# Down projection in seven products for 40 of 44 feature tiles, with a half piece last whose sums stay on chip, and all weight sums formed in memory during attention

## The chip, the core and the metric

The kernel runs on one core of a Trainium2 chip, in one launch. The metric is device microseconds of that core, lower is better. PE is the matrix engine, DVE the vector engine, ACT the scalar engine, POOL the GpSimd engine and SP the engine that here only issues transfers. All arithmetic is on 4-byte floats; each large product is made of three matmuls of split operands (below).

## The reference

One layer of a streaming encoder on x of 512 tokens by 2048 columns: a norm, a joint q/k/v projection, 16 attention heads of three kinds, an output projection with residual, a norm, a gated MLP of width 5632, a residual and a last norm. What the change touches is the last product:

```
    x = x + jnp.einsum('bse,ed->bsd', y, w_o[l])                    # attention's output, residual
    h = rmsnorm(x, ffn_norm[l])
    g = causal_dwconv(jnp.einsum('bsd,df->bsf', h, w_gate[l]), conv_w[l], conv_b[l])
    u = jnp.einsum('bsd,df->bsf', h, w_up[l])
    x = x + jnp.einsum('bsf,fd->bsd', jax.nn.silu(g) * u, w_down[l])   # "down", 5632 -> 2048
return rmsnorm(x, final_norm)
```

## The kernel before

**Split products.** Each operand is split into a high part (`wh`, a cast on ACT) and a remainder (`wl`, a subtraction on DVE). `mm3` (L67) makes a product of three matmuls: high by remainder, remainder by high, high by high. A "step" below is the work with one pair `wh`, `wl` of 128 by 1024 weights.

**Stages.** Attention runs 16 heads ("slots" 0 to 15). Each head ends in `finish`, which stores its output (`y_dram`) on POOL's queue. The output projection follows, then gate and up, tile by tile over 44 feature tiles, of which 40 use a seven-product scheme of their own (`strassen`), then down.

**Down.** The 44 feature tiles of 128 are 11 chunks of `CH` = 4. A *piece* of 4 chunks (2 pairs `b` of chunks) is multiplied in Strassen's manner: the 2 by 2 blocks are chunk of a pair by token half on the features' side, and chunk of a pair by column group `g`, `g+1` on the weights' side. Seven products `n` = 1 to 7 take the place of eight. The sums on the features' side are formed during gate/up and stored (`ab_dram`, `t_dram`); those on the weights' side are formed here. `NSEV` = 32 gives two pieces, and each is worked off in two *units* `Seven(c, g)`, `g` = 0 and 2. A unit has 14 products (7 `n` by 2 `b`) of two steps each, 28 steps, and a step has 12 matmuls of 512 columns (`multiply`).

**Order in this stage.** It is written by hand for all engines. In iteration `k`, `parts` casts and subtracts the weights of step `k`; between the cast and the subtraction stands `prepare(k+1)`, the addition (if any) that the next step's source needs; `prepare_6` forms the operand of product 6 (`s2`, tiles `sh`, `sl`); then come the matmuls of step `k`, and `sums(k)`, which reads finished accumulators. `wh` and `wl` have three buffers (`wspl`), so the cast of step `k` can start when step `k-3` is done. The raw weights have four buffers, in `rw` and `wraw`. Accumulators: `r1` and `r6` in the four `acc` banks, `r5` and `r7` in the four `att` banks, which the later products `dn` use as well.

**Weight sums.** Only the first unit (`self.formed`) finds sums ready-made, in `s_dram`: POOL's queue writes four tiles of 1 MB in attention, each by a copy (slots 0 to 3) and an accumulating transfer onto it (slots 4 to 7), memory to memory. The other three units add on DVE, eight additions each.

**Result sums.** `sums` builds each unit's four output blocks in tiles `e` and `U` (pool `ep`, one buffer each) and `put` stores them to one memory tensor per piece, `c_dram[0]` and `c_dram[1]`. Chunks 8 and 9 are then plain products (`down`, 192 matmuls of 512 columns each), added into the residual `x2` by `plus`. Between their groups of four output tiles the generator `turned` loads the stored sums of both pieces, adds them (DVE), transposes them on PE (16 transposes to a group) and adds them to `x2`. Chunk 10 is a plain product too, made in two token halves of 256 columns; the last norm of the first half runs under the second. `gated(c, n)` loads and splits a plain chunk's features (`ah`, `al`).

Of the kernel before, what the change touches and what calls it, by code (L numbers as in the profile page):

```python
# [24 lines left out]
NSEV = 32  # L25
# [18 lines left out]
def trunk(ctx, tc, xT, wqkv, wo, wo15, wgu, wd, par, lam4, rel, out):  # L44
# [72 lines left out]
    s_dram = [dram.tile([P, 2048], F32, name=f"s_dram{i}") for i in range(4)]  # L117
    c_dram = [dram.tile([P, NB, D], F32, name=f"c_dram{i}") for i in range(NSEV // 16)]
# [123 lines left out]
    with ExitStack() as actx:  # L242
# [172 lines left out]
        def finish(o, summer, n, eps, gain, slot):  # L415

            sq = tmp.tile([P, S], F32, tag="t2", name="osq")
            act.activation(sq, o, AF.Square)
# [13 lines left out]
            if slot >= KT - 2:  # L432
                pending.append(last)
            else:
                stored = pool.dma_start(y_dram[:, slot, :], o).ins
                if slot < 8:

                    i = slot % 4
                    b, w = divmod(i, 2)
# [55 lines left out]

        def chunk_pair(p, qkh, vs):
            ws = []
            for c in range(2):
                bias = tmp.tile([P, S], F32, tag="bias", name="rbias", bufs=2)
                pool.dma_start(bias, rel[2 * p + c])  # L500
# [3 lines left out]
                for i in reversed(range(NB)):  # L504
# [7 lines left out]
                    yield 2  # L512
            yield 3
# [163 lines left out]
        for n in range(NH - 2):  # L677
            if n == 7:
                far_masks()
            weave(n, following(n), 48, 8 if n == 0 else 0)  # L680
# [318 lines left out]
    with ExitStack() as actx:  # L999
# [52 lines left out]
        def features(c, i):  # L1052

            n, b = ORDER[i]
# [17 lines left out]
        def weights(src):  # L1072
            raws[0] += 1
            raw = (rw, wraw)[raws[0] % 2].tile([P, 2048], F32, tag="raw", name="raw")
            sync.dma_start(raw, src)
            return [raw.rearrange("p (m i c) -> p m i c", m=4, i=4)[:, :, 2 * h : 2 * h + 2, :] for h in range(2)]
# [4 lines left out]
        class Seven:  # L1081


            def __init__(self, c, g, fs):
                self.c, self.g, self.fs = c, g, fs
                self.banks, self.s2 = {}, {}
                self.formed = c == g == 0

            def load(self):
                c, g = self.c, self.g  # L1090
                w = {}
                for b in range(2):
                    w["11", b] = weights(wd[c + 2 * b, g])
                    if self.formed:
                        w["22", b], w["21", b] = [weights(s_dram[2 * b + s]) for s in range(2)]
                    else:
                        w["21", b], w["22", b] = [weights(wd[c + 2 * b + i, g + 1]) for i in range(2)]
                for b in range(2):
                    w["12", b], w["x22", b] = [weights(wd[c + 2 * b + 1, g + j]) for j in range(2)]
                self.w = w  # L1100

            def prepare(self, k):
# [3 lines left out]
                n, b = ORDER[k // 2]  # L1106
                h, w = k % 2, self.w
                a = {key: w[key, b][h] for key in ("11", "21", "22", "12", "x22")}
                if n in (1, 2, 4):
                    self.src = a[{1: "11", 2: "12", 4: "x22"}[n]]  # L1110
                elif n == 6:
                    self.src = self.s2[b][h]
                else:
                    s2 = self.s2[b][h] if n == 3 else None
                    dst, x, y = {
                        5: (a["22"], a["21"], a["22"]),
                        7: (a["21"], a["21"], a["11"]),
                        3: (s2, s2, a["12"]),
                    }[n]
                    if n == 3 or not self.formed:  # L1120
                        add(dst, x, y)
                    self.src = dst

            def prepare_6(self, k):

                n, b = ORDER[k // 2]
                h, w = k % 2, self.w
                if n == 7:
# [14 lines left out]
            def multiply(self, k):  # L1143
                n, b = ORDER[k // 2]
# [6 lines left out]
                for i in range(2):  # L1151
                    o, w = (2 * h + i) * HS, slice(i * S, (i + 1) * S)
                    for t in range(2):
# [6 lines left out]
                            b == h == i == 1,  # L1160
# [9 lines left out]

            def sums(self, k):

                r = self.banks
                if k == 12:
# [3 lines left out]
                elif k == 17:  # L1178
# [4 lines left out]
                elif k == 18:  # L1183
# [3 lines left out]
                elif k == 26:  # L1187
# [4 lines left out]
                elif k == 28:  # L1192
# [4 lines left out]
                elif k == 30:  # L1197
# [4 lines left out]
        c0 = NSEV // CH  # L1202
        NSTEP = 2 * len(ORDER)
        fs = [{} for _ in range(0, c0, 4)]
        units = [Seven(c, g, fs[c // 4]) for c in range(0, c0, 4) for g in (0, 2)]
# [4 lines left out]
        at = {s: (0, i) for i, s in FIRST.items()}  # L1210
        for n in range(1, len(fs)):
            at.update({(2 * n - 1) * NSTEP + s: (n, i) for i, s in NEXT.items()})
# [3 lines left out]
        def load_features():  # L1216
            if wanted:
                n, i = wanted.pop(0)
                loaded.append(features(4 * n, i))

        def split_features(n, i):
            fs[n][ORDER[i]] = feature_parts(i, loaded.pop(0))
# [14 lines left out]
        with tc.manual_schedule(engines={E.PE, E.DVE, E.Activation, E.SP, E.Pool}):  # L1237
# [4 lines left out]
            for s in range(len(units) * NSTEP + 3):  # L1242
                u, k = divmod(s, NSTEP)
                if u < len(units):
                    v, q = divmod(s + 1, NSTEP)
                    units[u].parts(lambda: units[v].prepare(q) if v < len(units) else None)
                    if v < len(units):
                        units[v].prepare_6(q)
                    units[u].multiply(k)
                if u > 0:  # L1250
                    units[u - 1].sums(k + NSTEP)
                if u < len(units):
                    units[u].sums(k)
                if s in at:
                    split_features(*at[s])
                    if at[s] > (0, 3):
                        load_features()
                if u == len(units) - 1 and k in (18, 21, 24, 26):
                    load_residual((18, 21, 24, 26).index(k))
# [5 lines left out]
        def turned():  # L1265

            yield
            for g in range(4):
                cs = []
                for c in c_dram:  # L1270
                    cs.append(rw.tile([P, NB, S], F32, tag="raw", name="cs"))
                    sync.dma_start(cs[-1], c[:, :, g * S : (g + 1) * S])
                for c in cs[1:]:
                    dve.tensor_tensor(out=cs[0], in0=cs[0], in1=c, op=ALU.add)
                for mm in range(4):
                    x = x2[4 * g + mm]
                    bank = acc_bank("ct")
                    for t in range(NB):
                        pe.transpose(
                            out=bank[:, t * P : (t + 1) * P], in_=cs[0][:, t, mm * P : (mm + 1) * P], identity=ident  # L1280
# [55 lines left out]

        kept = [pair(n, name="k") for n in range(8)]
# [74 lines left out]
```

## Time and profile before

| what | value |
|---|---|
| runs shown | 2204.95, 2206.73, 2207.64 us; median 2206.73 |
| the profiled execution | 2206.56 us, of which the span of its trace is 2204.8 and 1.76 lie outside the span |
| PE | busy 2173.9 us of the span, 99% |
| DVE, ACT, POOL | busy 73%, 49%, 13% |
| gate/up in seven products | 924.9 to 1741.1 us |
| down in seven products (4 units) | 1741.1 to 2049.7 us |
| down, plain chunks 8 and 9 | 2049.7 to 2143.8 us |
| down, chunk 10 in two halves | 2143.8 to 2190.4 us |
| the end (last norm, stores) | 2190.4 to 2204.8 us |

Times are positions in the span. A busy PE is a PE whose queue of matmuls doesn't run dry; the clock granted to it is 1.00 in every stage but the end. "Idle before, and what ended it" in a group names who was waited for.

### The profile page before, as it was taken

To read this page: it belongs to the slowest core of one execution; us is meant where nothing else is said; L and a number is where in the kernel's file an instruction comes from. 1 tells how busy PE (TensorE), PEld (TensorE's weight loads), DVE (VectorE), ACT (ScalarE), POOL (GpSimd) and SP (SyncE) were. 2 spreads that over 40 slices of the span, in tenths; PEclk is the share of its full clock that TensorE was granted. 3 is DMA by queue.
4 is the path that set the end of the run, shared out by engine and by line. 5 is a ranking of instruction groups with operands and counts; after the bars stand their busy time and mean duration, and the time that the engine had idled before them with its cause. 6 is when DMAs were issued, how large, how long until landed. Compare 5 with 4: busy or idle time off the path is not lost.

```text
span 2204.8 us, 34927 instructions
## 1 busy us (share of the span) xinstructions
PE 2173.9 (99%) x13916; PEld 1984.3 (90%) x13916; DVE 1604.0 (73%) x2277; ACT 1071.9 (49%) x1566; POOL 292.5 (13%) x531
## 2 busy tenths in 40 slices
PE   8999999999999999999999999999999999999997
PEld 7889888898888888799999999999999978888887
DVE  6665666877677547877777777787777788887675
ACT  5555555777565224444444444444444554544232
POOL 0100101000112221111111111111111010000003
PEclk9999999999999999999999999999999999999999
DMA  5332434222234445877787788778777665556742
GB/s 196 109 111 101 124 101 123 89 84 89 98 119 163 165 145 185 274 233 221 193 239 217 196 227 225 205 212 224 196 200 189 224 225 195 201 200 232 264 172 77
DMA packets 98163, 388.14 MB, mean 176 GB/s; under 512 B 11408, under 2 KB 20368, under 8 KB 81040
## 3 DMA queue, kind: packets, MB, share of 16 engines
q1 hardware_dynamic: 65728, 269.90, 35.9%
q0 software_dynamic: 30976, 114.84, 20.4%
q8 instruction: 109, 1.79, 0.3%
q10 hardware_dynamic: 1296, 1.17, 0.2%
q14 instruction: 54, 0.44, 0.1%
HBM read 341.30 MB, written 52.95 MB: 179 GB/s over the span
## 4 chain that ended last, share of the span: by engine, by line
PE 95%; DMA 2%; DVE 2%; issue 1%; ACT 0%; SPq 0%; DVEq 0%; POOLq 0%; ACTq 0%
PE c L67 36%; PE r L67 12%; PE v L67 8%; PE q L67 8%; PE k L67 8%; PE wo L67 8%; PE dn L67 6%; PE g L67 2%; PE u L67 2%; PE tr L395 1%; DMA f<-t_dram 1%; PE pv L67 1%; PE sc L360 1%; PE sc L359 1%; PE pv L410 0%
## 5 line engine op out<-in xcount | busy, mean ns | idle before, releaser
L61 DVE TENSOR_TENSOR wl<-a,wh 128x1024 fp32r<-128x1024 f32 x199 | 243.4, 1223 | 176.2 <-ACT wh L60 175.9
L67 PE MATMUL c<-bl,wh 128*128 128x256 f32 x1280 | 363.7, 284 | 4.3 <-ACT wh L60 4.3
L67 PE MATMUL c<-bh,wl 128*128 128x256 f32 x1280 | 363.6, 284 | 0.7 <-DVE wl L61 0.7
L67 PE MATMUL c<-bh,wh 128*128 128x256 f32 x1280 | 363.4, 284 | 0.0
L60 ACT CAST wh<-a 128x1024 fp32r<-128x1024 f32 x199 | 209.0, 1050 | 242.5 <-DVE a L873 207.2
L60 ACT CAST wh<-raw 128x1024 fp32r<-128x1024 f32 (+1 forms) x163 | 168.6, 1035 | 257.2 <-PE wo L67 88.7
L67 PE MATMUL c<-h2l,wh 128*128 128x256 f32 x960 | 272.0, 283 | 1.4 <-DVE U L899 0.9
L67 PE MATMUL c<-h2h,wh 128*128 128x256 f32 x960 | 271.8, 283 | 0.0
L67 PE MATMUL c<-h2h,wl 128*128 128x256 f32 x960 | 271.8, 283 | 0.0
L67 PEld LDWEIGHTS c<-bl,wh 128*128 128x128 f32 x1280 | 246.9, 193 | 4.6 <-ACT wh L60 4.5
L67 PEld LDWEIGHTS c<-bh,wl 128*128 128x128 f32 x1280 | 246.9, 193 | 1.0 <-DVE wl L61 1.0
L67 PEld LDWEIGHTS c<-bh,wh 128*128 128x128 f32 x1280 | 246.9, 193 | 0.0
L61 DVE TENSOR_TENSOR wl<-raw,wh 128x1024 fp32r<-128x1024 f32 (+1 forms) x163 | 197.0, 1211 | 64.8 <-ACT wh L60 64.2
L67 PEld LDWEIGHTS c<-h2l,wh 128*128 128x128 f32 x960 | 184.4, 192 | 1.8 <-DVE U L899 1.1
L67 PEld LDWEIGHTS c<-h2h,wl 128*128 128x128 f32 x960 | 184.4, 192 | 0.0
L67 PEld LDWEIGHTS c<-h2h,wh 128*128 128x128 f32 x960 | 184.4, 192 | 0.0
L67 PE MATMUL r<-wl,fh 128*128 128x512 f32 x448 | 174.8, 390 | 2.8 <-DVE wl L1140 2.8
L67 PE MATMUL r<-wh,fl 128*128 128x512 f32 x448 | 174.4, 389 | 0.0
L67 PE MATMUL r<-wh,fh 128*128 128x512 f32 x448 | 174.3, 389 | 0.0
L67 PE MATMUL v<-wl,hh 128*128 128x256 f32 x512 | 148.0, 289 | 8.2 <-DVE wl L61 8.2
L67 PE MATMUL v<-wh,hh 128*128 128x256 f32 x512 | 146.3, 286 | 0.0
L67 PE MATMUL v<-wh,hl 128*128 128x256 f32 x512 | 146.2, 286 | 0.0
(305 smaller groups left out, 5180.4 us busy)
## 6 DMA issues: line engine op xcount, KB each, us to landing
a<-in_wgu SPq DMA_DIRECT2D x121, 512.0 KB, 5.9
raw<-in_wd SPq DMA_DIRECT2D x48, 1024.0 KB, 5.7
raw<-in_wqkv SPq DMA_DIRECT2D x46, 1024.0 KB, 4.8
z<-in_wgu SPq DMA_DIRECT2D x80, 512.0 KB, 5.6
z<-in_wgu POOLq DMA_DIRECT2D x78, 512.0 KB, 9.3
raw<-in_wo SPq DMA_DIRECT2D x16, 1024.0 KB, 4.9
raw<-in_wgu SPq DMA_DIRECT2D x8, 1024.0 KB, 4.9
ab_dram<-g POOLq DMA_DIRECT2D x32, 256.0 KB, 6.4
```

The lines of the kernel that those rows point to most:

```text
L60: a = act.copy(out=hi, in_=src)
L61: d = dve.tensor_tensor(out=lo, in0=src, in1=hi.bitcast(F32), op=ALU.subtract)
L67: pe.matmul(o, l[x], r[y], start=start and i == 0, stop=stop and i == 2, skip_group_check=on)
L359: pe.matmul(bank[:, kt], q[c][:, qt], k[c][:, kt], start=True, stop=False)
L360: pe.matmul(bank[:, kt], q[c][:, qt], kh[c][:, kt], start=False, stop=not strict)
L395: pe.transpose(out=bank[:, (i - j) * P : (i - j + 1) * P], in_=w[:, o : o + P], identity=ident)
```

## The change

`NSEV` goes from 32 to 40: chunks 8 and 9 become a third piece with one pair of chunks (`nb` = 1), whose two units have 7 products, 14 steps each. The plain chunks are gone, and chunk 10 alone is left.

- **Weight sums.** All six units read their sums from `s_dram`, now 20 tiles. The copies are issued on ACT's queue, two in each of slots 0 to 9, and the accumulating transfers on POOL's queue, two in each of slots 2 to 11. The loads of the band heads' bias move from POOL's queue to ACT's and are issued ahead (`load_bias`). The additions in `prepare` for products 5 and 7 are gone; those for 6 and 3 stay.
- **Order of products.** With two pairs the last products go 2, 2, 3, 3, 4, 4 where they went 2, 3, 4, 2, 3, 4. With one pair the order is 1, 6, 5, 7, 2, 3, 4.
- **Result sums.** `c_dram` is one tensor; the second piece's `put` accumulates onto the first's. The half piece's units don't store: `load_sums` brings the sums so far into tiles `c_last`, and `last_sums` adds the accumulators to these, the first copy of `r1` on ACT.
- **End.** The weights of chunk 10's first group are loaded and split within the last unit. Two groups of transposes (32) run right behind the last unit, the other two between the groups of chunk 10's first half.

```diff
-NSEV = 32
+NSEV = 40
...
+    s_parts = {}
+    for c in range(0, NSEV // CH, 2):
+        for g in (0, 2):
+            s_parts[c, g, 1] = (c + 1, g + 1), (c, g + 1)
+            s_parts[c, g, 3] = (c, g), (c, g + 1)
...
+                keys = list(s_parts)
+                with tc.issue_after(squared):
+                    for key in keys[2 * slot : 2 * slot + 2]:
+                        act.dma_start(s_dram[key], wd[s_parts[key][0]])
+                if slot >= 2:
                     with tc.issue_after(stored):
-                        if slot < 4:
-                            pool.dma_start(s_dram[i], wd[2 * b, 0] if w else wd[2 * b + 1, 1])
-                        else:
-                            pool.dma_start(s_dram[i], wd[2 * b, 1], accum_op=ALU.add, max_dma_last_dim=8192)
+                        for key in keys[2 * slot - 4 : 2 * slot - 2]:
+                            pool.dma_start(s_dram[key], wd[s_parts[key][1]], accum_op=ALU.add, max_dma_last_dim=8192)
...
-        ORDER = [(n, b) for b in range(2) for n in (1, 5, 7, 6)] + [(n, b) for b in range(2) for n in (2, 3, 4)]
+        def order_of(nb):
+            first = (1, 6, 5, 7) if nb == 1 else (1, 5, 7, 6)
+            return [(n, b) for b in range(nb) for n in first] + [(n, b) for n in (2, 3, 4) for b in range(nb)]
+
+        PIECES = [(c, min(4, NSEV // CH - c) // 2) for c in range(0, NSEV // CH, 4)]
...
+                self.read = dict(zip((12, 17, 18, 23, 27, 30), range(6)))
...
-                if n in (1, 2, 4):
-                    self.src = a[{1: "11", 2: "12", 4: "x22"}[n]]
-                elif n == 6:
+                if n == 6:
                     self.src = self.s2[b][h]
+                elif n == 3:
+                    s2 = self.s2[b][h]
+                    add(s2, s2, w["12", b][h])
+                    self.src = s2
                 else:
...
-                    if n == 3 or not self.formed:
-                        add(dst, x, y)
-                    self.src = dst
+                    self.src = w[{1: "11", 2: "12", 4: "x22", 5: "22", 7: "21"}[n], b][h]
...
-                pool.dma_start(c_dram[self.c // 4][:, 2 * t : 2 * t + 2, col], e)
+                pool.dma_start(c_dram[:, 2 * t : 2 * t + 2, col], e, accum_op=ALU.add if self.c else ALU.bypass)
...
+            def load_sums(self, row):
+
+                g = self.g + row
+                for t, e in reversed(list(enumerate(pair((1, 2, 3, 9)[g], F32, "c")))):
+                    c_last[g, t] = e.rearrange("p (t c) -> p t c", t=2)
+                    pool.dma_start(c_last[g, t], c_dram[:, 2 * t : 2 * t + 2, g * S : (g + 1) * S])
+
+            def last_sums(self, k):
+                r = self.banks
+
+                def onto(row, t, n=None):
+                    e = c_last[self.g + row, t]
+                    if n is None:
+                        add(e, self.U, e)
+                    else:
+                        for i in range(2):
+                            add(e[:, i, :], r[n][i], e[:, i, :])
+
+                if k == 2:
+                    self.U = fe.tile([P, 2, S], F32, tag="f", name="U")
+                    for i in range(2):
+                        act.copy(out=self.U[:, i, :], in_=r["1"][i])
+                elif k == 4:
+                    for i in range(2):
+                        add(self.U[:, i, :], r["6"][i], self.U[:, i, :])
+                sums = {
+                    5: (1, 1),
+                    6: (1, 1, "5"),
+                    7: (0, 1),
+                    8: (1, 1, "7"),
+                    9: (1, 0),
+                    12: (0, 0, "1"),
+                    13: (0, 1, "5"),
+                    14: (1, 0, "7"),
+                }
+                if k in sums:
+                    onto(*sums[k])
...
+                if u == len(units) - 1 and k == 4:
+                    kept[0] = [pair(n, name="k") for n in (5, 6)]
+                    raw_last = next_raw(wd[NCH - 1, 0])
+                if u == len(units) - 1 and k in (12, 13):
+                    split(*kept[0][k - 12], raw_last[:, (k - 12) * 1024 : (k - 11) * 1024])
...
-            yield
             for g in range(4):
-                cs = []
-                for c in c_dram:
-                    cs.append(rw.tile([P, NB, S], F32, tag="raw", name="cs"))
-                    sync.dma_start(cs[-1], c[:, :, g * S : (g + 1) * S])
-                for c in cs[1:]:
-                    dve.tensor_tensor(out=cs[0], in0=cs[0], in1=c, op=ALU.add)
+                cs = c_last[g, 0], c_last[g, 1]
...
-        a = gated(c0, 14)
-        for c in range(c0, NCH - 1):
-            down((load_unit(wd[c, g]) for g in range(4)), a, plus, between=rest)
-            a = gated(c + 1, 8 if c == c0 else 14)
+        a = gated(NCH - 1, 14)
...
+        next(rest)
+        next(rest)
+        down((load_unit(wd[NCH - 1, g], kept[g]) if g else kept[0] for g in range(4)), a, squares, t0, rest)
+        down([kept[g] for g in range(4)], a, squares, t1, last_norm(t0, (sync,)))
```

How the instructions stand on the engines, at three places.

POOL, in the head of slot 4: `y_dram` is the store of the head's output, `mx` the negated row maxima that the next head's softmax waits for, `rl` and `rh` zeroed tiles. Before:

```order
L435 DMA y_dram_80<-o_2536 128x512
L444 DMA s_dram0_85<-in_wd 128x2048
L385 TENSOR_SCALAR mx_2680<-mx_2680 128x1
L385 TENSOR_SCALAR mx_2687<-mx_2687 128x1
L385 TENSOR_SCALAR mx_2716<-mx_2716 128x1
```

After the change, at the same store:

```order
L441 DMA y_dram_80<-o_2559 128x512
L450 DMA s_dram2_0_1_89<-in_wd 128x2048
L450 DMA s_dram2_0_3_90<-in_wd 128x2048
L391 TENSOR_SCALAR mx_2713<-mx_2713 128x1
L391 TENSOR_SCALAR mx_2742<-mx_2742 128x1
L391 TENSOR_SCALAR mx_2749<-mx_2749 128x1
```

There are two accumulating transfers between the store and the next `mx` where there was one.

DVE, in the first unit, steps 17 to 19: `wl` are remainders, `c` and `U` the result sums read from the accumulators `r`, `sl` an addition for product 3. Before:

```order
L1140 TENSOR_TENSOR wl_18535<-raw_18181,wh_18534 128x4x2x128
L1079 TENSOR_TENSOR U_18449<-r6_18317,U_18449 128x512
L1079 TENSOR_TENSOR c_18551<-r5_18235,U_18449 128x512
L1079 TENSOR_TENSOR U_18449<-r6_18318,U_18449 128x512
L1079 TENSOR_TENSOR c_18551<-r5_18236,U_18449 128x512
L1079 TENSOR_TENSOR sl_18258<-sl_18258,raw_18181 128x1024
L1140 TENSOR_TENSOR wl_18557<-sh_18257,wh_18556 128x4x2x128
```

After the change:

```order
L1158 TENSOR_TENSOR wl_18614<-raw_18260,wh_18613 128x4x2x128
L1103 TENSOR_TENSOR U_18528<-r6_18396,U_18528 128x512
L1103 TENSOR_TENSOR c_18629<-r5_18314,U_18528 128x512
L1103 TENSOR_TENSOR U_18528<-r6_18397,U_18528 128x512
L1103 TENSOR_TENSOR c_18629<-r5_18315,U_18528 128x512
L1158 TENSOR_TENSOR wl_18635<-raw_18262,wh_18634 128x4x2x128
```

The addition `sl` between the four sums and the next remainder is gone from this place; it now stands some steps later.

DVE in the first unit of the half piece, steps 8 to 11, which has no counterpart before (`cl`, `ch` are tiles of `c_last`, `sh` and `sl` the additions for product 3):

```order
L1158 TENSOR_TENSOR wl_20658<-raw_20476,wh_20657 128x4x2x128
L1103 TENSOR_TENSOR cl_20420<-r7_20616,cl_20420 128x512
L1103 TENSOR_TENSOR cl_20420<-r7_20617,cl_20420 128x512
L1103 TENSOR_TENSOR sh_20481<-sh_20481,raw_20476 128x1024
L1158 TENSOR_TENSOR wl_20676<-raw_20476,wh_20675 128x4x2x128
L1103 TENSOR_TENSOR ch_20419<-U_20556,ch_20419 128x1024
L1103 TENSOR_TENSOR sl_20482<-sl_20482,raw_20476 128x1024
L1158 TENSOR_TENSOR wl_20694<-sh_20481,wh_20693 128x4x2x128
```

The remainders of steps 9 and 10 (the second and third `wl`) stand behind sums from accumulators that the step just before them has closed.

## Rows read from the trace of the kernel before

**Rows 1.** The page, part 1: the span, then for each engine busy microseconds, share of the span and number of instructions.
```profile
span 2204.8 us, 34927 instructions
...
PE 2173.9 (99%) x13916; PEld 1984.3 (90%) x13916; DVE 1604.0 (73%) x2277; ACT 1071.9 (49%) x1566; POOL 292.5 (13%) x531
```

**Rows 2.** The three longest waits of PE in the whole program: who waited for whom, microseconds in total, how often, the longest.
```profile
PE v L67 <- DVE wl L61: 8.2, 2, 6.3
PE c L67 <- ACT wh L60: 4.3, 1, 4.3
PE r L67 <- DVE wl L1140: 2.8, 3, 1.5
```

**Rows 3.** Stretches of the program, in order of the text: attention, the split gate/up products, the seven-product units of the down projection, its two plain chunks, its last chunk in two token halves, the end. Columns: the stretch, its length, busy time (and instructions) of each engine, granted clock, mean busy share of the DMA engines, GB/s.
```profile
60.00:650.00 590.00, 590.00 (x3476) 523.00 (x3475) 411.08 (x859) 353.49 (x691) 58.72 (x168) 1.00 0.31 103
924.90:1741.10 816.20, 809.83 (x6722) 808.88 (x6721) 612.60 (x709) 374.20 (x445) 124.23 (x191) 1.00 0.77 212
1741.10:2049.70 308.60, 305.83 (x1347) 252.18 (x1346) 252.76 (x239) 153.06 (x158) 28.60 (x48) 1.00 0.62 223
2049.70:2143.80 94.10, 94.10 (x449) 78.85 (x448) 67.57 (x78) 24.81 (x24) 0.74 (x1) 1.00 0.61 217
2143.80:2190.40 46.60, 46.60 (x388) 46.45 (x386) 26.71 (x57) 16.06 (x36) 21.13 (x28) 1.00 0.14 46
2190.40:2204.80 14.40, 0.84 (x4) 0.30 (x2) 8.73 (x22) 1.66 (x4) 0.00 (x0) 0.63 0.44 146
```

**Rows 4.** A PE group behind the seven-product stage: the transposes of the stored sums; count | busy, mean ns of one | idle before.
```profile
L1279 PE MATMUL ct<-ident,cs 128*128 128x128 f32 x64 | 7.6, 272 | 0.0
```

**Rows 5.** Timeline of the seven-product stage: start us, duration, engine, line, operation [idle before <- releaser]. First a wait of PE in the first unit; then the first matmuls of two consecutive steps of the last unit (2036.12 and 2038.84) with one conversion on ACT and one remainder on DVE.
```profile
1791.84 0.39 PE L67 MATMUL r<-wh,fh 128*128 128x512 f32 x1
1793.72 0.50 PE L67 MATMUL r<-wl,fh 128*128 128x512 f32 x1 [1.49 <-DVE wl L1140]
1794.06 0.40 PE L67 MATMUL r<-wh,fl 128*128 128x512 f32 x1
...
2036.12 0.39 PE L67 MATMUL r<-wl,fh 128*128 128x512 f32 x1
...
2036.37 1.05 ACT L1138 CAST wh<-sl 128x1024 fp32r<-128x1024 f32 x1 [1.66 <-PE r L67]
...
2037.45 1.22 DVE L1140 TENSOR_TENSOR wl<-sl,wh 128x1024 fp32r<-128x1024 f32 x1 [1.49 <-ACT wh L1138]
...
2038.84 0.39 PE L67 MATMUL r<-wl,fh 128*128 128x512 f32 x1
```

**Rows 6.** Timeline of DVE in the first unit, at the wait of rows 5: the last of four additions from PSUM, an addition of two weight blocks, a remainder.
```profile
1790.71 0.69 DVE L1079 TENSOR_TENSOR c<-r,U 128x512 f32<-128x512 f32 x1
1791.32 1.22 DVE L1079 TENSOR_TENSOR sl<-sl,raw 128x1024 f32<-128x1024 f32 x1
1792.45 1.22 DVE L1140 TENSOR_TENSOR wl<-sh,wh 128x1024 fp32r<-128x1024 f32 x1
```

**Rows 7.** Groups of DVE and (last row) of ACT in the seven-product stage: count | busy, mean ns of one | idle before, and what ended it.
```profile
L1140 DVE TENSOR_TENSOR wl<-raw,wh 128x1024 fp32r<-128x1024 f32 x78 | 95.2, 1222 | 31.0 <-ACT wh L1138 30.8
...
L1079 DVE TENSOR_TENSOR raw<-raw 128x1024 f32<-128x1024 f32 x24 | 29.3, 1220 | 0.4 <-DMA raw<-in_wd 0.4
...
L1079 DVE TENSOR_TENSOR c<-r,U 128x512 f32<-128x512 f32 x16 | 10.7, 687 | 2.6 <-DMA c_dram<-c 2.3
...
L1177 ACT COPY U<-r 128x512 f32<-128x512 f32 x8 | 4.3, 583 | 0.0
```

**Rows 8.** Timeline of DVE: two of the additions of transposed sums from PSUM into the residual.
```profile
2072.29 1.27 DVE L1282 TENSOR_TENSOR xh<-xh,ct 128x512 f32<-128x512 f32 x2
```

**Rows 9.** Microseconds from issue to landing (least, median, most), a row for each source line. In turn: the sums put into memory in the seven-product stage (L1166, 512 KB, 16 of them), the accumulating transfers of gate/up weights (L858, 512 KB, 78), the accumulating memory-to-memory transfers of attention (L444, 1 MB, 4), the plain memory-to-memory copies of attention (L442, 1 MB, 4), the weight loads during attention (L72, 1 MB, 43).
```profile
DMA to landing us min/median/max: 3.1/3.3/8.8
...
DMA to landing us min/median/max: 6.0/9.3/12.2
...
DMA to landing us min/median/max: 8.5/9.5/10.3
...
DMA to landing us min/median/max: 6.0/6.0/6.0
...
DMA to landing us min/median/max: 4.7/4.9/9.4
```

**Rows 10.** Timeline in attention: one weight load issued by SP, and two later conversions of weight halves on ACT. The halves converted at 175.94 (not shown) and 183.47 lie in the other buffer, so the loaded unit is first read by the conversion at 190.29.
```profile
172.51 0.33 SPq L72 DMA_DIRECT2D raw<-in_wqkv  x1
...
183.47 1.06 ACT L60 CAST wh<-raw 128x1024 fp32r<-128x1024 f32 x1 [3.10 <-PE q L67]
...
190.29 1.03 ACT L60 CAST wh<-raw 128x1024 fp32r<-128x1024 f32 x1
```

**Rows 11.** Timeline of POOL: around one accumulating memory-to-memory transfer in attention, and two accumulating transfers in a row in gate/up.
```profile
261.86 0.93 POOL L444 DMA_DIRECT2D s_dram<-in_wd  x1
262.91 0.21 POOL L385 TENSOR_SCALAR mx<-mx 128x1 f32<-128x1 f32 x1
...
1531.85 1.73 POOL L858 DMA_DIRECT2D z<-in_wgu  x2 [0.50 <-ACT wh L60]
```

**Rows 12.** Timeline in the same head: the last block of softmax weights on DVE and the transposes on PE that read it.
```profile
273.70 0.35 DVE L466 SCALAR_TENSOR_TENSOR w<-pr,r 128x128 f32<-128x128 f32 x1
...
279.74 0.60 PE L395 MATMUL tr<-ident,w 128*128 128x128 f32 x4
```

More of the change, by code (lines that the diff above doesn't have):

```diff
@@ L115, in trunk @@
     a_dram = dram.tile([P, NFT - NSEV, S], F32, name="a_dram")
-    s_dram = [dram.tile([P, 2048], F32, name=f"s_dram{i}") for i in range(4)]
-    c_dram = [dram.tile([P, NB, D], F32, name=f"c_dram{i}") for i in range(NSEV // 16)]
+    s_parts = {}
[3 more added lines that the diff above has]
+            s_parts[c, g, 3] = (c, g), (c, g + 1)
+    s_dram = {key: dram.tile([P, 2048], F32, name="s_dram%d_%d_%d" % key) for key in s_parts}
+    c_dram = dram.tile([P, NB, D], F32, name="c_dram")
     b_dram = dram.tile([P, KT // 2, 4, S // 2], F32, name="b_dram")
@@ L494, in pair_out, with load_bias @@
             yield from finish(o, pair1, HD, NORM_EPS, gain, slot)
+        biases, rels = [], [rel[i] for i in range(8)]
+        def load_bias():
+            if rels:
+                biases.append(tmp.tile([P, S], F32, tag="bias", name="rbias", bufs=2))
+                act.dma_start(biases[-1], rels.pop(0))
         def chunk_pair(p, qkh, vs):
@@ L1091, in load @@
                 w = {}
-                for b in range(2):
+                for b in range(self.nb):
                     w["11", b] = weights(wd[c + 2 * b, g])
[L1094 to L1099, printed above, removed]
+                    w["22", b], w["21", b] = [weights(s_dram[c + 2 * b, g, n]) for n in (1, 3)]
+                for j, name in enumerate(("12", "x22")):
+                    for b in range(self.nb):
+                        w[name, b] = weights(wd[c + 2 * b + 1, g + j])
                 self.w = w
@@ L1241, in trunk @@
             units[0].prepare(0)
[L1242 to L1249, printed above, removed]
-                if u > 0:
[L1251 to L1256, printed above, removed]
-                        load_features()
-                if u == len(units) - 1 and k in (18, 21, 24, 26):
-                    load_residual((18, 21, 24, 26).index(k))
+            kept = {}
+            steps = [(u, k) for u in range(len(units)) for k in range(units[u].nstep)]
+            for s in range(len(steps)):
+                u, k = steps[s]
+                v, q = steps[s + 1] if s + 1 < len(steps) else (None, None)
+                units[u].parts(lambda: units[v].prepare(q) if v is not None else None)
+                if v is not None:
+                    units[v].prepare_6(q)
+                units[u].multiply(k)
+                if u > 0:
+                    units[u - 1].sums(k + units[u - 1].nstep)
+                units[u].sums(k)
+                if (u, k) in last_loads:
+                    for row in last_loads[u, k][1]:
+                        units[last_loads[u, k][0]].load_sums(row)
+                if (u, k) in at:
+                    split_features(*at[u, k])
+                    if at[u, k] > (0, 3):
+                        load_features()
+                if u == len(units) - 1 and k == 4:
[3 more added lines that the diff above has]
+                    split(*kept[0][k - 12], raw_last[:, (k - 12) * 1024 : (k - 11) * 1024])
+                if u == len(units) - 1 and k in (4, 6, 8, 11):
+                    load_residual((4, 6, 8, 11).index(k))
+            for k in range(3):
+                units[-1].sums(k + units[-1].nstep)
         def plus(m, t, bank):
```

88 lines of the change are left out of this document (43 added, 45 removed).

## The prediction, made before the changed kernel was timed

> **What bounds the kernel now.** I began with the page's busy times: PE works 2173.9 of 2204.8 us [rows 1], so only fewer matmuls or fewer gaps between them can help. Then the waits of PE: the longest come to 8.2 and 4.3 us and lie in other stages, and those in the seven-product units to 2.8 in all [rows 2]. Then the table by stage [rows 3]: in 1741.1 to 2049.7 PE is busy 305.83 of 308.60 us and DVE 252.76 (82%); in the plain chunks PE is busy for the whole 94.10. So each matmul less in these stages is time gained, unless PE starts to wait, and the engine nearest to making it wait is DVE.
>
> **Term 1, matmuls.** The four units of before make 4 × 28 × 12 = 1344 matmuls, 305.83/1344 = 0.2275 us each [rows 3]. The two plain chunks have 2 × 192 = 384 of the same size; what is left of their 94.10 us, 94.10 - 384 × 0.2275 = 6.7, is the 64 transposes of [rows 4], 0.105 each (the 272 ns shown for one overlap). The transposes stay 64. In place of 384 matmuls stand two units of 14 × 12 = 168, together 336. So 48 go: -48 × 0.2275 = **-10.9**.
>
> **Term 2, new waits in the half piece.** A full step lasts 2.72 us (2036.12 to 2038.84), its cast takes 1.05 and its remainder 1.22 [rows 5]; additions in a row go at 1.13 (1791.32 to 1792.45) [rows 6]; a sum from an accumulator takes 0.69 on DVE and 0.58 for ACT's copy [rows 7]. The last write of a bank is readable some 0.25 behind the step (the cast at 2036.37, released by PE, starts 0.25 behind 2036.12, where one step ends and the next starts). With one pair, a product's accumulator closes two steps before its reader stands on the engine, not ten. Let S be the start of the step named:
> - Step 3: the second copy of `r1` runs S2+0.25 to 0.83, then ACT casts to 1.88, DVE subtracts to 3.10, where 2.72 is the due time: 0.4 late.
> - Step 9: the second `r7` sum ends at S8+0.94, the addition for product 3 at 2.07, the remainder at 3.29: 0.6 late.
> - Step 10: behind that remainder stand the addition of `U` (1.13), one more for product 3 (1.13) and the next remainder (1.22). It ends at S8+6.7, where S9+2.72 = S8+6.0: 0.7 late.
>
> That is 1.7 in a unit. A PE that had waited takes 0.34 for its first matmul (1793.72 to 1794.06 [rows 5]) where 0.23 is usual, 0.1 each for three waits. So 2.0 a unit, **+4.0** for two. What is late next: step 11's remainder ends 1.22 behind step 10's, well ahead of its due time. Bounds: 0, if the sums land sooner than I place them and these chains just fit, and +6, if a further step in each unit is as late.
>
> **Term 3, straight into transposes.** Before, the transposes stood between groups of plain products and hid the additions that empty their banks. Now 32 run at once, behind the last step, T. Four banks take 16 of them; the fifth bank waits for DVE, which has the second `r7` sum until T+0.94, then two additions per 1.27 us [rows 8], 0.64 each. The fourth addition ends at T+3.5, the last four transposes (0.42) at about T+4.3 with the 0.25 of a semaphore, where 32 × 0.105 = 3.4 would do: **+0.9**. Bounds: 0, if the products of chunk 10 slip in without a gap, and +3.3, if the two remainders of chunk 10's features (1.22 each) still stand ahead of these sums.
>
> **Term 4, the full units.** Additions of weight blocks cost DVE 24 × 1.22 = 29.3 us before [rows 7], but PE's waits for remainders of this stage, 2.8 us, are three, and the one whose cause I followed is in the first unit, which had no such additions. So their going is worth 0 (at most 1). In the first unit PE waited 1.49 at 1793.72 because an addition stood between four sums and a remainder [rows 5, 6]. That addition now stands a few steps later, where feature splits stand too. I take 0, with bounds -1.5 (the wait goes) and +1.5 (it comes back there).
>
> **Costed at nothing, with their cover.**
> - Weight loads: the units read as many tiles as before, 1 MB each, from `s_dram` in place of `in_wd`.
> - Attention's transfers: 16 more copies (6.0) and 16 more accumulations (9.5) [rows 9], at most 248 us of transfer over 590 us with a DMA share of 0.31 [rows 3], which would bring it to 0.73. A weight load issued at 172.51 is first read at 190.29 [rows 10], 17.8 us later, while its landing takes 4.9, at most 9.4 [rows 9]; that is the cover. If it were gone, each unit's first matmul would wait.
> - Two accumulating issues in a row on POOL: one takes 0.93 and the next row maximum follows at once; two took 1.73 in gate/up [rows 11]. So maxima come 0.8 later. In the head with such a transfer the softmax weights are done at 274.05 and read at 279.74 [rows 12]: 5.7 us of slack.
> - Feature sums of eight more tiles, formed in gate/up: 32 of 40 tiles have them before, and PE is busy there for 809.83 of 816.20 us [rows 3]. Of the rest, 4.3 us is one wait for a cast [rows 2]. If the cover were gone, each of the eight tiles would wait.
> - ACT's two issues a head, 0.33 each by SP's [rows 10], beside an ACT that is busy 353 of 590 us [rows 3].
>
> The Trainium skill, page "DMA: Bandwidth & Descriptors", section "Issuing engines are not separate DMA queues", says that transfers of SP, ACT and POOL run on the same 16 engines and interleave, so spreading the issues saves issue time alone. The trace bears it out: the same weight load has a median of 4.9 and a maximum of 9.4 [rows 9]. By that rule the sum stays as it is while no more than two transfers lie beside a load; what it would do beyond that is way two of rival D.
>
> **Sum.** -10.9 + 4.0 + 0.9 + 0 = -6.0. Of the profiled execution's 2206.56 (span 2204.8 [rows 1] and 1.76 outside it) that leaves **2200.6**; the median of the runs shown, 2206.73, is 0.17 above that execution, so the change is -0.28%. A measurement can tell about 0.2%, 4.4 us: faster is under 2202.3, slower over 2211.1.
>
> **Rivals.**
> - *A. The waits don't come.* The chains of term 2 miss by only 0.4 to 0.7 us. If a bank is read sooner than I place it, or one of the additions finds an earlier gap, half of the waits or all of them go, and term 3's with them: -10.9 + 0 to 2, which is 2196 to 2198. Against it: the instructions stand in that order, and their lengths are measured.
> - *B. Accumulating stores come late.* A plain store of result sums lands in 3.3 (median) [rows 9]. An accumulating one is in no row of this stage; from below it costs the plain 3.3, and by the ratio of attention's transfers (9.5 to 6.0) 5.2; from above, the accumulating loads of gate/up take 9.3 and at most 12.2. I take 5.2 to 9.3. Tile `e` is wanted again four steps, 10.9 us, after its store, and the additions into it stand ahead of a remainder. Before, DVE already waited 2.3 us for such stores, unseen by PE [rows 7]. A store of 9.3 is hidden; one of 13 makes PE lose 2.1 us in each of the second piece's two units, +4; one of 15, 4.1 in each, +8. So 2205 to 2209.
> - *C. More waits in the half piece.* DVE carries more in a half-piece unit than in a full one: all bounds at the top, -10.9 + 6 + 3.3 + 1.5 = -0.1, about 2206.
> - *D. Attention stalls, and the kernel is slower.* Way one: if POOL can't finish the second accumulating issue until the first has landed, the row maxima behind it come 9.5 us late [rows 9]. Then 9.5 - 5.7 [rows 12] = 3.8 us are lost, in the six or seven heads in which maxima follow the pair: +23, about 2223. It decides against the change when the block exceeds 5.7 + 6.0/6 = 6.7 us. Against it: in gate/up two such transfers in a row took 1.73 to issue [rows 11], though of half the size. Way two: a weight load meets two copies, two accumulations and the store or a bias load, and takes five shares, 5 × 4.9 = 24.5 us [rows 9]; it would miss its 17.8 [rows 10] by 6.7, and twice in each of two heads would give +27. At three shares, 14.7, nothing is late. That is the mechanism of the rule cited above.
>
> **Chances and range.** Forecast 0.55, A 0.10, B 0.15, C 0.10, D 0.10 (0.07 by way one, 0.03 by way two, for which the longest load seen is 9.4). The forecast's own range is 2198 to 2203. Faster: A and nine tenths of the forecast, 0.60. Slower: D and a little of B, 0.12. No difference: the rest, 0.28. For 8 in 10 the range takes in A from 2196.5 up and C and the lower half of B; it ends at 2208 and leaves D out.
>
> **What would show it.** Term 1: the seven-product stage with six units ends near 2130 (2049.7 + 336 × 0.2275 + 4.0), the first 32 transposes near 2134, chunk 10 with the other 32 near 2184 (2134.4 + 46.6 + 3.4), and the span 14.4 later [rows 3]. Term 2: PE waits for `wl` at three places in each of the last two units, 0.4 to 0.7 each. Term 3: a wait of PE for `ct` additions just behind the last unit. Term 4: at 1793 no wait, at most one a few steps later. B: the landing of the stores onto `c_dram` in the third and fourth unit, over 11 if B is right. D: waits of PE in the heads from slot 2 on, behind row maxima or behind weight loads. The prediction is wrong if attention's stretch grows by more than 2 us, or if PE waits over 10 us in the seven-product units.

## The result: slower by 0.28%, and the profile after

The changed kernel takes 2212.61 us (median of 18 runs, 2208.41 to 2217.17) where the kernel before takes 2206.73 (median of 18): ratio 1.0028, 95% interval 1.0021 to 1.0035. I had forecast 2200.6 and a range up to 2208.0; the result lies outside it, on the other side. The runs of the changed kernel spread over 9 us, those of before over 4. The profiled execution took 2212.66, with a span of 2210.9.

The page of the changed kernel, part 1 (as in [rows 1]):

```profile
span 2210.9 us, 34934 instructions
...
PE 2169.5 (98%) x13868; PEld 1976.2 (89%) x13868; DVE 1598.5 (72%) x2286; ACT 1087.5 (49%) x1585; POOL 326.5 (15%) x558
```

PE has its 48 instructions less, and is busy 4.4 us less, not 10.9; the span is longer. The table by stage (columns as in [rows 3]; the seven-product stage now holds six units, and the fourth row is the 32 transposes behind it) shows where:

```profile
60.00:650.00 590.00, 582.50 (x3414) 515.67 (x3413) 394.38 (x831) 342.86 (x671) 68.53 (x170) 0.99 0.52 157
936.90:1754.10 817.20, 809.90 (x6721) 808.96 (x6720) 617.83 (x725) 374.44 (x445) 131.09 (x199) 1.00 0.78 216
1754.10:2142.40 388.30, 384.28 (x1683) 314.50 (x1682) 300.23 (x289) 191.19 (x197) 43.00 (x64) 1.00 0.65 221
2142.40:2146.20 3.80, 3.80 (x33) 3.35 (x32) 3.80 (x7) 1.79 (x2) 0.00 (x0) 1.00 1.01 416
2146.20:2196.40 50.20, 50.20 (x421) 49.96 (x419) 36.65 (x71) 17.97 (x39) 23.09 (x28) 1.00 0.19 64
2196.40:2210.90 14.50, 0.72 (x3) 0.30 (x2) 8.60 (x22) 1.66 (x4) 0.00 (x0) 0.64 0.44 145
```

Down, from 1754.1 on, lasts 456.8 us; before it was 1741.1 to 2204.8, 463.7 [rows 3]. It gained 6.9, a little more than the 6.0 of my sum. Gate/up's seven products take 1.0 more. But they start at 936.9 in place of 924.9 [rows 3]: **12.0 us are lost ahead of them**, and the first row shows that it happened in attention, where PE had been busy for 590.00 of 590.00 us and now is for 582.50, at a mean clock of 0.99. The longest waits of PE (as [rows 2]):

```profile
PE v L67 <- DVE wl L61: 10.7, 3, 6.0
PE c L67 <- ACT wh L60: 5.2, 1, 5.2
PE tr L401 <- DVE mx L381: 4.3, 1, 4.3
PE r L67 <- DVE wl L1158: 3.9, 10, 1.0
```

`v` waits three times in place of two, and `tr` is new. Both places in the timeline, with what DVE, ACT and POOL do there:

```profile
508.74 0.34 ACTq L507 DMA_DIRECT2D rbias<-in_rel  x1
...
519.32 0.11 DVE L513 MEMSET rbias<- 64x64 f32 x1 [3.99 <-DMA rbias<-in_rel]
...
529.92 0.39 PE L67 MATMUL v<-wl,hh 128*128 128x256 f32 x1 [2.33 <-DVE wl L61]
...
553.58 1.82 POOL L450 DMA_DIRECT2D s_dram<-in_wd  x2
...
557.43 0.34 ACTq L507 DMA_DIRECT2D rbias<-in_rel  x1
...
565.74 0.39 PE L67 MATMUL k<-hh,wl 128*128 128x512 f32 x1
565.97 0.39 PE L67 MATMUL k<-hh,wh 128*128 128x512 f32 x1
...
569.26 0.11 DVE L513 MEMSET rbias<- 64x64 f32 x1 [10.73 <-DMA rbias<-in_rel]
...
570.67 0.47 PE L401 MATMUL tr<-ident,w 128*128 128x128 f32 x1 [4.32 <-DVE mx L381]
...
571.38 0.63 PE L67 MATMUL k<-hh,wl 128*128 128x512 f32 x1
571.80 0.63 PE L67 MATMUL k<-hh,wh 128*128 128x512 f32 x1
```

A bias load of 256 KB is issued 3.9 us behind a pair of accumulating transfers of 1 MB each. The first instruction that needs the bias, a small fill of its masked corner, stands next on DVE; DVE works in order, and so everything behind the fill waits 10.73 us for the load. At 508.74 the same happens, with 3.99. (By the order of their starts in the two traces, this second fill stands where it stood before the change, with the same number of DVE instructions ahead of it; the third, at 569.26, stands 17 places earlier.) PE runs out of work twice, for 2.33 and 4.32 us. And behind the second wait, the matmuls of 512 columns start 0.42 us apart, where just ahead of it they started 0.23 apart (1.2 in place of 2.4 GHz). The granted clock by stretches (stretch, length, PE busy and instructions, clock, DMA share, GB/s; the last one begins where the second wait ends):

```profile
520.00:530.00 10.00, 7.67 (x40) 1.00 0.32 104
530.00:540.00 10.00, 10.00 (x69) 0.83 0.30 105
...
560.00:570.00 10.00, 6.36 (x29) 0.95 0.98 267
570.00:580.00 10.00, 9.33 (x37) 0.71 0.18 48
570.67:580.00 9.33, 9.33 (x37) 0.73 0.19 51
```

Behind the first wait the low clock costs 0.17 × 10 = 1.7 us, behind the second 0.27 × 9.33 = 2.5; the rest of the second low stretch, in 560 to 570.67, lies in the wait itself, where it slows no matmul. With the waits, 2.33 + 4.32 and two of 0.42 in other heads, that is 11.7 of the 12.0 us. The bias loads' landing times (least, median, most), which before the change were 2.9, 3.3 and 5.2:

```profile
DMA to landing us min/median/max: 2.6/3.8/11.7
```

### The profile page after: what moved, and what is told of

Read it like the earlier page. It is cut to its first block, busy times and chain, and to the rows that moved or that the text cites. A ratio compares the mean times of both kernels' runs of the same rounds, so it can differ in the third digit from the quotient of the medians.

```text
span 2210.9 us, 34934 instructions
## 1 busy us (share of the span) xinstructions
PE 2169.5 (98%) x13868; PEld 1976.2 (89%) x13868; DVE 1598.5 (72%) x2286; ACT 1087.5 (49%) x1585; POOL 326.5 (15%) x558
## 4 chain that ended last, share of the span: by engine, by line
PE 89%; DVE 4%; DMA 4%; issue 2%; ACT 1%; SPq 0%; DVEq 0%; ACTq 0%; POOLq 0%
PE c L67 36%; PE r L67 14%; PE v L67 8%; PE wo L67 8%; PE k L67 7%; PE q L67 7%; PE dn L67 2%; PE tr L401 1%; DMA rbias<-in_rel 1%; DMA f<-ab_dram 1%; PE pv L67 1%; PE sc L366 1%; PE sc L365 1%; DVE wl L1158 1%; DMA xt<-x_dram 1%
## 5 line engine op out<-in xcount | busy, mean ns | idle before, releaser
L60 ACT CAST wh<-raw 128x1024 fp32r<-128x1024 f32 (+1 forms) x147 | 151.8, 1033 | 184.3 <-PE wo L67 86.8
L61 DVE TENSOR_TENSOR wl<-raw,wh 128x1024 fp32r<-128x1024 f32 (+1 forms) x147 | 177.2, 1209 | 86.4 <-ACT wh L60 85.8
L67 PE MATMUL r<-wl,fh 128*128 128x512 f32 x560 | 219.2, 391 | 4.0 <-DVE wl L1158 3.9
L67 PE MATMUL r<-wh,fl 128*128 128x512 f32 x560 | 218.0, 389 | 0.0
L67 PE MATMUL r<-wh,fh 128*128 128x512 f32 x560 | 217.9, 389 | 0.0
L1156 ACT CAST wh<-raw 128x1024 fp32r<-128x1024 f32 x100 | 105.3, 1054 | 119.5 <-PE r L67 111.5
L1158 DVE TENSOR_TENSOR wl<-raw,wh 128x1024 fp32r<-128x1024 f32 x100 | 122.2, 1222 | 49.6 <-ACT wh L1156 49.5
```

The source lines that it names most:

```text
L60: a = act.copy(out=hi, in_=src)
L61: d = dve.tensor_tensor(out=lo, in0=src, in1=hi.bitcast(F32), op=ALU.subtract)
L67: pe.matmul(o, l[x], r[y], start=start and i == 0, stop=stop and i == 2, skip_group_check=on)
L1156: act.copy(out=hv, in_=src)
L1158: dve.tensor_tensor(out=lv, in0=src, in1=hv.bitcast(F32), op=ALU.subtract)
```

## The experiments

Theory 1 was what these rows suggest: bias loads share the DMA engines with the accumulating transfers, DVE stands still at the fill, and PE pays with a wait and a low clock. Theory 2: the traffic in attention as a whole, or ACT's issues. Theory 3: POOL's issues delay the row maxima. Each ratio is to runs of the kernel before on the same chip.

**Take the traffic away, leave the order.**

```diff
-                            pool.dma_start(s_dram[key], wd[s_parts[key][1]], accum_op=...)
+                            q = slice(0, P if slot < 10 else 8)
+                            pool.dma_start(s_dram[key][q], wd[s_parts[key][1]][q], accum_op=...)
```

> The changed kernel, but the accumulating transfers of slots 10 and 11 (the last 4 of 20) carry 8 of 128 rows each, so their sums are incomplete; order of instructions unchanged. Theory 1 (two bias loads share the DMA engines with these transfers, and DVE stands still at the fill of their tiles): the bias loads issued near 509 and 557 us land in 3 to 5 us in place of 10.5 and 11.7, PE's waits of 2.3 and 4.3 us in attention and the low clock behind them go, gate/up starts near 837 in place of 849, and the time is 2200 to 2202. Theory 2 (attention is slowed by the traffic as a whole, or by ACT's issues, of which all stay): 2210 to 2213. Theory 3 (POOL's blocked issues delay the row maxima): half of the loss goes at most, 2206 to 2210.

2202.46 us, ratio 0.9981 (0.9972 to 0.9989). That is 0.5 above what theory 1 had expected, and far from the others. The two waits are gone; attention's stretch has PE busy for 589.09 us, and no bias load takes more than 7.3:

```profile
60.00:650.00 590.00, 589.09 (x3467) 1.00 0.49 152
```

Four of twenty accumulating transfers carry the loss; the other sixteen and all twenty copies cost PE no more than two waits of 0.42. DVE still stands still for 4.00 us at the fill near 559, and PE does not wait for it: a stall of DVE costs time only beyond the lead that DVE has there.

**Leave the traffic, move the fill.**

```diff
-                dve.memset(bias[0:HD, S - HD : S], NEG)
+                with tc.issue_after(mark):      # mark: DVE's last transposes' split of the head before
+                    dve.memset(bias[0:HD, S - HD : S], NEG)
```

> The changed kernel with all its transfers; only the fill of the masked corner of a bias tile on DVE is held back behind the last transposes' split of the head before, so that DVE has work while the bias lands. Theory 1: the bias loads near 509 and 557 still land in 10 to 12 us, but DVE no longer stands still for 4 and 10.7 us, PE's waits in attention go from 7.5 to under 2 us, time 2200 to 2203. Theory 2 (traffic as a whole): nothing changes, 2210 to 2213, with PE waiting for weights elsewhere.

2202.12 us, ratio 0.9978 (0.9969 to 0.9987). Attention's stretch and the landing of the bias loads:

```profile
60.00:650.00 590.00, 589.15 (x3470) 1.00 0.53 160
...
DMA to landing us min/median/max: 2.6/4.1/12.0
```

A bias load still takes up to 12.0 us, and the DMA share is as high as in the changed kernel; yet the waits are gone, since DVE has other work in front of the fill (no fill waits for its load here). So it takes both, the late load and the fill that stands too early in an in-order engine. Theory 2 falls.

**Half a dose: only the last pair small** (`slot < 11` in the first diff).

> The changed kernel, but only the last pair of accumulating transfers (slot 11) is cut to 8 of 128 rows, so that two sums are incomplete; the pair of slot 10 stays, and the order of instructions. Theory 1, a half dose: the bias load near 557 lands in 3 to 5 us and its wait of 4.3 us goes with the low clock behind it (4.3 + 3.4 = 7.7); the load near 509 still takes 10 us, and PE's wait of 2.3 stays with some 1.7 of low clock. Time 2204.5 to 2206.5. If one of the two waits carries all of the loss: 2202 or 2212.

2207.11 us, ratio 1.0001 (0.9992 to 1.0010). The wait of 4.3 is gone, the other stays:

```profile
529.52 0.39 PE L67 MATMUL v<-wl,hh 128*128 128x256 f32 x1 [2.40 <-DVE wl L61]
```

From 2212.6 over 2207.1 to 2202.5: the second pair is worth 5.5 and the first 4.6 in the medians, where I had worked out 7.7 and 4.0. The time is 0.6 above what I had expected; the order of the two holds. The 7.7 was too high: it counted the low clock within the wait a second time, and without that it is 4.3 + 2.5 = 6.8.

**The loads on POOL's queue again** (`pool.dma_start(biases[-1], ...)`).

> The changed kernel with the bias loads issued on POOL's queue, as before the change, all transfers kept. If the engines behind the queues are what is shared, a bias load beside two accumulating transfers lands late on either queue, 8 to 15 us. The time depends on where the fill then stands on DVE: the order puts the third fill some 30 places later than in the changed kernel, the second some 12 later, so the 10.7 us stall shrinks and the time is 2202 to 2208. If ACT's queue is what made the loads late: they land in 3 to 5 us, time 2200 to 2202.

2202.34 us, ratio 0.9977 (0.9968 to 0.9986). The loads land as late as in the changed kernel, or later:

```profile
DMA to landing us min/median/max: 2.9/5.0/16.7
```

But in this order the fills stand later on DVE. The one that had cost 3.99 us now costs nothing, the one that had cost 10.73 costs 0.89, and the next one 3.03, which had cost nothing:

```profile
569.32 0.11 DVE L513 MEMSET rbias<- 64x64 f32 x1 [0.89 <-DMA rbias<-in_rel]
572.47 0.11 DVE L513 MEMSET rbias<- 64x64 f32 x1 [3.03 <-DMA rbias<-in_rel]
```

ACT's queue was not the cause. Here the loads stand behind the pair in POOL's own queue, which could make them late too; but in the first experiment they stayed on ACT's queue, with all of its copies, and none took over 7.3. The rule from the Trainium skill, page "DMA: Bandwidth & Descriptors", section "Issuing engines are not separate DMA queues", fits here: whatever engine issues them, transfers share the same engines.

**Three transfers a slot, all of them before slot 9.**

```diff
-                    for key in keys[2 * slot : 2 * slot + 2]:
+                    for key in keys[3 * slot : 3 * slot + 3]:
...
-                        for key in keys[2 * slot - 4 : 2 * slot - 2]:
+                        for key in keys[3 * slot - 6 : 3 * slot - 3]:
```

> The changed kernel with copies three in each of slots 0 to 6 and accumulating transfers three in each of slots 2 to 8, so that none lies beside the bias loads near 509 and 557 us; the same bytes in all. Theory 1: waits of PE in attention under 2 us, time 2199 to 2202, faster than both kernels. Theory 2 (traffic as a whole, now denser): 2211 or more. Theory 3 (row maxima behind POOL's issues): three in a row make it worse, 2212 or more, with waits of PE in slots 3 to 9.

2214.51 us, ratio 1.0036 (1.0023 to 1.0049). A miss: I had moved the traffic away from two bias loads and onto the first one. It was issued at 363.66 and took 11.0 us:

```profile
185.68 2.65 POOL L450 DMA_DIRECT2D s_dram<-in_wd  x3
...
200.17 0.44 PE L401 MATMUL tr<-ident,w 128*128 128x128 f32 x2 [1.84 <-DVE w L472]
...
374.68 0.11 DVE L513 MEMSET rbias<- 64x64 f32 x1 [8.93 <-DMA rbias<-in_rel]
...
375.39 0.80 PE L67 MATMUL pv<-rl,v 128*128 128x512 f32 x1 [4.64 <-DVE rl L61]
```

The last two rows are theory 1 at another place. The first two are new waits, for softmax weights (four in two heads, 4.8 us in all), in heads behind three issues in a row on POOL. Theory 3 expected waits there, but POOL does not hold them up: it works off three row maxima at 187.39, right behind its issues. The exponentials that need them stand on ACT behind a cast that waited for PE:

```profile
187.39 1.54 POOL L391 TENSOR_SCALAR mx<-mx 128x1 f32<-128x1 f32 x3
...
195.57 1.05 ACT L60 CAST wh<-raw 128x1024 fp32r<-128x1024 f32 x1 [3.31 <-PE k L67]
...
197.15 0.62 ACT L392 ACTIVATE pr<-pr,mx 128x384 f32<-128x384 f32 x1
```

In the changed kernel the exponentials of this head stand ahead of that cast (191.51 and 195.24), and PE doesn't wait. So the order on ACT moved here as well; why it did is not shown.

**Attention's part alone, on the kernel before** (its `finish`, `s_parts` and `load_bias`; down reads four of the 20 tiles).

> The kernel before with the change's attention part alone: 20 sums formed in memory by the same transfers at the same places, bias loads on ACT's queue; down is that of before and reads four of the sums. If attention carries the whole loss (12 us) and down gained its 6.9: 2217 to 2220. If down's part of the change costs some of the loss: under 2212.

2218.52 us, ratio 1.0055 (1.0043 to 1.0068): 11.8 us slower, with the same two waits:

```profile
530.94 0.38 PE L67 MATMUL v<-wl,hh 128*128 128x256 f32 x1 [2.44 <-DVE wl L61]
570.22 0.47 PE L400 MATMUL tr<-ident,w 128*128 128x128 f32 x1 [4.34 <-DVE mx L380]
```

**Down's part alone** (attention as before; five units add on DVE).

> The change in the down projection alone: 40 tiles in seven products, with attention's transfers and bias loads as in the kernel before, so only the first unit finds its sums formed and the five others add on DVE. If down gains what the stages of the changed kernel show (463.6 to 456.7, 6.9 us) and the additions on DVE are hidden: 2199 to 2201. If the sums formed in memory are what makes room on DVE for the half piece: new waits on remainders in the last two units, 2203 to 2207.

2204.93 us, ratio 0.9992 (0.9983 to 1.0001): no difference clear of noise. The two half-piece units take 82.6 us, where they take 79.8 in the changed kernel. The half piece's product 6 lacked an addend in this kernel, so I made it whole:

```diff
+                    if self.nb == 1:
+                        add(w["22", b][h], w["21", b][h], w["22", b][h])
                     add(self.s2[b][h], w["22", b][h], w["11", b][h])
```

> As e5_down_alone, which formed the operand of product 6 in the half piece from a block that still lacked an addend; here the sum of the two blocks is made first, two additions ahead of product 6 (in steps 0 and 1) in place of those ahead of product 5. The same number of additions on DVE. If the additions are what costs e5_down_alone its gain: PE's waits for remainders in the last two units are again more than three each, at steps near the additions, and the time is 2203 to 2206. If only their place did: 2200 to 2202.

2208.54 us, ratio 1.0007 (0.9998 to 1.0016), over my upper end. PE waits six times in the first half-piece unit in place of three, the first and longest where the additions for product 6 now stand:

```profile
2052.01 0.50 PE L67 MATMUL r<-wl,fh 128*128 128x512 f32 x1 [2.85 <-DVE wl L1153]
2062.23 0.50 PE L67 MATMUL r<-wl,fh 128*128 128x512 f32 x1 [0.16 <-DVE wl L1153]
2068.34 0.50 PE L67 MATMUL r<-wl,fh 128*128 128x512 f32 x1 [0.33 <-DVE wl L1153]
...
2083.97 0.50 PE L67 MATMUL r<-wl,fh 128*128 128x512 f32 x1 [0.39 <-DVE wl L1153]
```

The two half-piece units take 85.6 us. So neither half of the change gained by itself: at the two places tried, the additions on DVE take from the half piece what it gains, and the sums formed in memory, where they were put, cost more than it gains. Whether the additions could stand where they cost nothing is not tested.

**Both faults mended.** The fill held back as above, and the half piece's sums a step later:

```diff
-                if k == 2:
+                if k == 3:
...
-                elif k == 4:
+                elif k == 5:
...
-                    5: (1, 1),
-                    6: (1, 1, "5"),
-                    7: (0, 1),
-                    8: (1, 1, "7"),
-                    9: (1, 0),
+                    6: (1, 1),
+                    7: (1, 1, "5"),
+                    8: (0, 1),
+                    9: (1, 1, "7"),
+                    11: (1, 0),
```

> As e3_fill_later, and the half piece's sums from the first accumulator one step later (steps 3, 5, 6, 7, 8, 9 and 11 in place of 2, 4, 5, 6, 7, 8 and 9), so that no remainder stands behind a sum of the step just before. If the three waits in each of the last two units come from that order (0.16, 0.33 and 0.39 us with 0.1 for each restart): all six go, and the time is 2 to 2.5 us under that of e3_fill_later, 2199.5 to 2200.5. If the waits come from DVE being full: they move to other steps, same time as e3_fill_later.

2199.46 us, ratio 0.9961 (0.9948 to 0.9975): faster than both kernels, and 2.7 under the kernel with the fill alone (which ran on another chip; the ratios are 0.9961 and 0.9978). The six waits are gone; one new one comes behind the last step, where the transposes wait for DVE:

```profile
2131.97 0.44 PE L1347 MATMUL ct<-ident,ch 128*128 128x128 f32 x2 [1.18 <-DVE xh L1350]
```

## Why the prediction was wrong

**The step that failed** is "costed at nothing, with their cover", in two of its lines. I priced the 32 added transfers against the weight loads, whose cover of 17.8 us held (their longest landing rose to 12.5), and against POOL's issues. I did not price them against the other loads of the same stretch. The bias loads had no such cover: DVE came to the fill 6.6 us behind the issue of one load and 1.1 us behind that of the other (519.32 - 3.99 - 508.74 and 569.26 - 10.73 - 557.43), and they took 10.5 and 11.7 to land. And the bias loads' move to ACT's queue has no line of its own: ACT's issues I charged with 0.33 us each, but no load's landing beside the pair. [rows 9] held the warning: a weight load beside one accumulating transfer had already taken 9.4. The sign that I had named came: attention's stretch grew by more than 2 us, and what follows it starts 12.0 later. Rival D had the right place and sign, but both of its ways had another victim, and twice the price. And the prediction had no term for the clock, 4.2 of the 12.0 us. The kernel before could have told of one: its table by stage shows 1.00 up to the end, but that is a mean over long stages, and behind its wait of 4.31 in gate/up the granted clock was low there too:

```profile
930.00:940.00 10.00, 5.01 (x26) 4.52 (x25) 8.65 (x9) 4.68 (x6) 0.82 (x2) 0.73 0.97 339
```

**Term 1** (-10.9) and **term 2** (+4.0) held. The two half-piece units take 79.8 us (2062.67 to the end at 2142.46), 3.6 over 28 steps of 2.72; in the mended kernel two such units take 76.2. The waits are at the three steps named:

```profile
2071.15 0.50 PE L67 MATMUL r<-wl,fh 128*128 128x512 f32 x1 [0.16 <-DVE wl L1158]
2088.12 0.50 PE L67 MATMUL r<-wl,fh 128*128 128x512 f32 x1 [0.33 <-DVE wl L1158]
2091.53 0.50 PE L67 MATMUL r<-wl,fh 128*128 128x512 f32 x1 [0.39 <-DVE wl L1158]
```

They read 0.9 in a unit, not 1.7, but a unit loses 1.8: the restart behind a wait costs some 0.3, not 0.1. A wait is counted from the end of a matmul's 0.39 us, while matmuls start every 0.23, so 0.16 is lost beside the slow first matmul. That the term came out right is luck: two errors that cancel.

**Term 3** (+0.9): the 32 transposes took 3.74 us (2142.46 to 2146.20) where 3.4 would do: +0.3. With the sums later (the last experiment) it rises to 5.29, with the wait of 1.18 in it.

**Term 4** (0): the four full units take 308.5 us as before (1754.19 to 2062.67), with four short waits in the first in place of three.

**Rival B** did not come: the accumulating stores of result sums, those of the third and fourth unit, landed within the 5.2 to 9.3 that I took but for the longest:

```profile
DMA to landing us min/median/max: 6.1/6.6/9.8
```

**Gate/up** (costed at nothing) took 1.0 more here, and 0.0 to 2.7 more in the other profiles with the half piece. In all of these, and in the kernel before, PE waits between 930 and 955 us, where ACT waits for tiles reloaded from memory and the DMA engines are 85 to 100% busy; the wait is 4.31 long before and 2.33 to 6.26 in the others. A low clock follows it: the four profiles with 2.1 to 2.7 more have a mean granted clock of 0.85 over 925 to 960 us, the others and the kernel before 0.90, a difference of 1.7 us. Why the wait differs from run to run is open.

## What to carry to other kernels

A transfer that is "hidden" has to be weighed against every load that is in flight beside it, the small ones first: a load's cover is the distance in the in-order queue from its issue to its first reader, and a reader that stands right behind the issue has none. Price a gap on PE at the gap and the slow matmuls behind it. And before adding cover or traffic for a stage, ask whether the part that it serves needs it: here the half piece gained nothing clear of noise without the sums in the two kernels tried, and the sums cost next to nothing once the fills stood some instructions later on DVE.

## What I had not expected of the hardware

Waits of 2.33 and 4.32 us on PE were followed by stretches at a granted clock of 0.83 over 10 us and 0.73 over 9.33, which cost 1.7 and 2.5 us; waits of 0.2 to 1.0 in the seven-product units left the clock at 1.00. It is no fixed price: with attention's part on the kernel before, the wait of 2.44 at the same place left the clock at 1.00 from 530 to 550 us. A load of 256 KB, 3.3 us by itself, took 10.5 to 16.7 us beside two accumulating transfers of 1 MB (and a weight load), on whichever queue it was issued.
